# New TensorE prices in a kernel's list scheduler: weight loads counted, durations changed

## The chip, the cores and the metric

The kernel runs on one core of one Trainium2 chip. The time is device microseconds of one execution: the median of three runs before the change is 1827.13 us, with 1824.09 us the lowest and 1828.31 us the highest. Beside the runs there is one profiled execution, whose trace gives every instruction's start and length on each engine: TensorE (PE in the profile, its weight loads PEld), VectorE (DVE), ScalarE (ACT), GpSimd (POOL) and SyncE (SP), which issues all DMA transfers.

## What is computed

One inference step of one encoder layer, on a prompt of 2048 rows and on 8 samples of 16 rows (2176 rows in all), in float32. Cut to what matters:

```python
def mixer_layer(x, mk, mv, shift_prev, rwkv_s0, fox_past, p):
    h = rms_norm(x, norm_g) @ w_in                       # 1024 -> 3654 columns
    fox_cols, rwkv_cols, mem_cols = jnp.split(h, ...)
    o_f = fox_prompt(q, k, v, logf)   # 6 heads x 64, causal, forget gates' running sum on the logits
                                      # (fox_sample: 512 cached rows and 16 new ones)
    xs = token_shift(rwkv_cols, shift_prev, rwkv_mu)
    o_r, s_new, g_r = rwkv_branch(xs, rwkv_s0, ...)  # 6 heads x 64, S <- S diag(w) + S(-kk)^T(a kk) + v^T k
    o_m = mem_attend(mq, mem_q_g, mk, mv)            # 4 heads x 64 into 256 memory rows
    o = jnp.concatenate([o_f * silu(g_f), o_r * silu(g_r), o_m * silu(g_m)], -1)
    return x + o @ w_out, k, v, logf, s_new, rwkv_cols[:, -1:]
```

Outputs are the new rows, the attention keys, values and log forget gates, the memory keys and values, the recurrent states and the last projected rows.

## The kernel before

The work has two stages. The first one (pools `p1`) projects: in four blocks of 512 rows (the first one with the 128 sample rows) it normalises the rows, splits them in a rounded high part and a remainder, and multiplies by the input weights, split likewise, with three products for each pair (tiles `pjd` and `pjt`, 128 rows by 256 to 512 columns, type float32r). Among these products runs the recurrent branch in chunks of 64 rows: small float32 products that use the array in tiles of 64 x 64 or 32 x 32 (`gr`, `gw`, `gx`, `pz`, `pa`), and a chain of 8 steps for each pair of heads and block in which TensorE and VectorE alternate (`sc`, `st`). A plain float32 product makes two passes over the array.

The second one (pools `p2`) attends: for each pair of heads and 512 queries it turns queries and keys (`pt`, transposes on TensorE), finds row maxima (`pm`), computes scores (`pS`), takes the exponent on ScalarE (`P`), splits it (`Ph` on ScalarE, `Pl` on GpSimd) and multiplies by the values (`po`). On the diagonal blocks a bf16 product of a mask with the identity (`idb`) is added to `pm` and `pS`. The samples' attention (`sA` to `sD`, products of 16 columns among them) and the output projection (`py`) are spread among these steps as filler. All of that is in one Python program that only sets which instructions there are.

Their order is not that of the program. `_arrange` (called at the kernel's end) reads all instructions, gives each one a price (`_Op`), and runs a list scheduler (`_schedule`) 18 times: three weights in `_TRIES`, six rounds each, in which the ranks are moved towards the middle between a node's earliest and latest start. The order with the least planned total is taken, for all five engines and so for the order of the DMA transfers on SyncE too. At each step the scheduler takes, over all engines, the candidate with the least key. For TensorE the key comes from `_Array.starts`, a model of the array: it knows the shape of the tiling in use (`self.shape`), when each tile of it is free (`self.free`), a change of tiling (`_TURN`, 92 ns), and a half-clock state (`slow`) in which a product takes twice as long, decided by the work counted in ticks of 3.4 us (`cells`, `_WARM`). `_Array.run` then books the product and says when its result is there. Products of the small tilings that can be run together are one node, a visit (`_visits`). ScalarE, VectorE and GpSimd instructions have a price `time` until the result is seen and `own` until the next one may start; `shares` and `two` say which VectorE instructions wait for GpSimd's at the shared port. A product's times are `own` and, before the change, `time`; in `_Problem.length` and below it `own` also enters the ranks.

Of the kernel before, what the change touches and what calls it, by code (L numbers as in the profile page):

```python
# [1466 lines left out]
_TURN = 92  # L1467
_TICK = 10240 / 3
# [9 lines left out]
class _Pools:  # L1478


    def __init__(self, tc):
        self.tc, self.open, self.below = tc, [], {}
# [10 lines left out]
def _free(dims):  # L1493
    n = 1
    for _, k in dims[1:]:
        n *= k
    return n
# [46 lines left out]
class _Op:  # L1544


    def __init__(self, i, eng):
        ins, outs = ([s.bass_ap for s in x if getattr(s, "bass_ap", None) is not None] for x in (i.ins, i.outs))
        aps, kind = ins + outs, type(i).__name__
        space = lambda a: str(getattr(a.tensor, "_space", ""))  # L1550
        sizes = [_free(list(a.ap)) for a in ins]
        n = max(_free(list(a.ap)) for a in aps)
        self.shares = self.reads = self.two = False
        if eng == "PE":
            x, w = ins[:2]
            wide = str(i.ins[0].dtype) == "dt.float32"
            rows, cols, self.n = list(x.ap)[0][1], sizes[1], sizes[0]
            self.turns, self.plain, self.bf = i.is_transpose, wide and not i.is_transpose, "bf" in str(i.ins[0].dtype)
            size = lambda k: 32 if k <= 32 else 64 if k <= 64 else 128
            self.shape = (size(rows), size(cols)) if self.plain else (128, 128)  # L1560
            self.place = tuple(i.tile_position or (0, 0))
            self.load = 2 * cols / 2.4
            self.cells = self.n * rows / 128 * ((2 if self.turns else 4) if wide else 1)
            if self.plain:
                self.own = 2 * max(cols, self.n) / 1.2 + (10 if rows > 64 else 2)
                self.time = self.own + 165
            else:
                self.own = 30 if self.turns else 40 if self.bf else max(3 + 0.4453 * self.n, 12 + 0.4219 * self.n)
                self.time = 275 if self.turns else self.n / 2.4 + 170
            return  # L1570
        psum = any("PSUM" in space(a) for a in aps)
        scalar = n > 1 and any(k == 1 for k in sizes)
        if eng == "SP":
            size = 4 * list(outs[0].ap)[0][1] * _free(list(outs[0].ap))
            run = min(4 * list(a.ap)[-1][1] if list(a.ap)[-1][0] == 1 else 4 for a in aps)
            self.own, self.wire = (430 if run < 512 else 360), size / 230
            self.time = 1300 + (size / 140 - size / 230) * (run < 1024) / 2
            return
        wide = sum(k > 1 and "SB" in space(a) for k, a in zip(sizes, ins))
        self.reads = wide > 0  # L1580
        if eng == "Activation":
            t = (140 if psum else 178) + 0.833 * n + 90 * scalar
        elif eng == "Pool":
            if "pow" in str(getattr(i, "op", "")):
                t = 360 + 163 * n
            elif "Memset" in kind:
                t = 95 + 0.83 * n
            elif "ScalarPtr" in kind:
                t = 210 + 1.09 * n if n > 256 else 190 + 2.1 * n
            else:  # L1590
                t = 200 + 2.13 * n
        else:
            self.two = not psum and sum(k > 1 for k in sizes) == 1 and ("TensorCopy" in kind or "TensorScalar" in kind)
            self.shares = self.two or wide > 1
            if "Memset" in kind:
                t = max(65, 57 + 1.04 * n)
            elif "Reciprocal" in kind:
                t = 148 + 6.3 * n
            elif "Custom" in kind:
                t = 220 + 1.042 * n  # L1600
            else:
                t = 155 + 0.521 * n if self.two else 152 + 1.042 * n + 52 * (scalar and "ScalarPtr" in kind)
        self.time, self.own = t, t - _BACK[eng]
# [79 lines left out]
class _Array:  # L1683


    def __init__(self):
        self.shape, self.free, self.base, self.last, self.turned, self.cells = None, {}, 0, -1e9, -1e9, {}

    def slow(self, x):
        t = int(x // _TICK)  # L1690
        return 1 if t < 3 or self.cells.get(t - 1, 0) >= _WARM else 2

    def starts(self, c, ready):

        if c.shape == self.shape:
            plain = max(ready, self.base, self.free.get(c.place, 0) if c.shape != (128, 128) else self.free.get(0, 0),
                        self.last + 3)
            if c.turns:
                plain = max(plain, self.turned + 109)
            return plain, plain  # L1700
        plain = max(ready, max(self.free.values(), default=0), self.base)
        return max(ready, max(self.free.values(), default=0) + _TURN, self.base), plain

    def run(self, c, ready):
        s, _ = self.starts(c, ready)
        place = c.place if c.shape != (128, 128) else 0
        w = self.slow(s)
        own = c.own * w
        if c.shape != self.shape:
            self.shape, self.free, self.base = c.shape, {}, s  # L1710
        if c.plain and place not in self.free:
            own += c.load * w
        if c.turns:
            self.turned = s
        self.free[place], self.last = s + own, s
        t0, t1 = s / _TICK, (s + max(own, 1)) / _TICK
# [312 lines left out]
```

## Time and profile before

| | |
|---|---|
| median of three runs | 1827.13 us (1824.09 to 1828.31) |
| profiled execution | 1826.43 us, its span 1824.6 us |
| granted TensorE clock, mean | 0.967 |
| busy: TensorE, weight loads | 1756.1 us (96%), 1395.2 us (76%) |
| busy: VectorE, ScalarE, GpSimd | 927.2, 895.5, 793.7 us |
| DMA | 292.42 MB, mean 160 GB/s |

The span runs from the first to the last instruction; the rest of the execution's time lies around it. TensorE's products are pipelined and their ends in the trace are modelled, so two of them overlap in it and a busy TensorE need not be at its peak: how much a product takes of the engine is read from the distance between starts. The granted clock is 1.0 at full speed and 0.5 at half.

### The profile page before, as it was taken

Reading aid. Unit: us, or ns where it says so; the run is one execution under the profiler, and the core shown is the slowest. Engines: PE = TensorE matmul, PEld = TensorE weight load, DVE = VectorE, ACT = ScalarE, POOL = GpSimd, SP = SyncE. Lnnn points to the kernel's source line nnn. Section 1 sums busy time; section 2 is a strip of 40 time slices with the busy share of each in tenths; the row PEclk is TensorE's granted clock in tenths of the full one; section 3 lists DMA queues with packets and bytes.
Section 4 is the critical chain, followed back from the end, with each engine's and each line's share of the span. In section 5 each row is a group of like instructions: output and inputs, shape, how many; then the busy total and the mean of one; then the engine's idle time right before and its main releaser. Section 6 shows DMA issues by size and latency. Waiting matters only on the chain.

```text
span 1824.6 us, 41978 instructions
## 1 busy us (share of the span) xinstructions
PE 1756.1 (96%) x16883; PEld 1395.2 (76%) x16883; DVE 927.2 (51%) x2102; ACT 895.5 (49%) x1755; POOL 793.7 (43%) x818
## 2 busy tenths in 40 slices
PE   7999999999999999998999998999999999999998
PEld 6998999788877888876788886666666566667776
DVE  5544444464445553545743453767455545575213
ACT  5424343524234323324332434887888477986452
POOL 4555342242131341311332152567676265876452
PEclk8999999999999999999999999899999589999999
DMA  6767463745446464535363353434437542354422
GB/s 193 242 206 242 138 203 113 240 164 174 139 153 203 148 220 163 161 102 178 108 220 131 124 156 120 155 117 156 152 124 242 181 160 87 124 174 145 159 99 97
DMA packets 208905, 292.42 MB, mean 160 GB/s; under 512 B 56844, under 2 KB 161790, under 8 KB 192838
## 3 DMA queue, kind: packets, MB, share of 16 engines
q1 hardware_dynamic: 208710, 289.73, 48.5%
q8 instruction: 133, 2.18, 0.5%
q14 instruction: 62, 0.51, 0.1%
HBM read 202.58 MB, written 87.08 MB: 159 GB/s over the span
## 4 chain that ended last, share of the span: by engine, by line
PE 79%; DVE 7%; ACT 5%; DMA 3%; issue 3%; SPq 1%; POOL 1%; DVEq 0%; ACTq 0%; POOLq 0%
PE pjd L59 20%; PE pjt L59 12%; PE py L59 10%; PE po L59 9%; PE pS L59 7%; PE pm L59 4%; PE sc L59 2%; PE sy L59 1%; PE gr L59 1%; PE pz L59 1%; PE pa L59 1%; PE spr L59 1%; DMA w<-w_d 1%; PE gw L59 1%; PE gx L59 1%
## 5 line engine op out<-in xcount | busy, mean ns | idle before, releaser
L59 PE MATMUL pjd<-xk,w 128*128 128x512 f32 (+4 forms) x2280 | 522.6, 373 | 8.9 <-DVE xk L62 4.1
L59 PEld LDWEIGHTS pjd<-xk,w 128*128 128x128 f32 (+1 forms) x2280 | 380.4, 190 | 75.6 <-issue 10.2
L62 POOL TENSOR_TENSOR Pl<-P,Ph 128x512 fp32r<-128x512 f32 (+3 forms) x272 | 315.4, 1170 | 158.5 <-ACT Ph L1137 122.2
L59 PE MATMUL pjt<-w,xk 128*128 128x256 f32 x2040 | 282.4, 290 | 6.8 <-issue 3.5
L59 PEld LDWEIGHTS pjt<-w,xk 128*128 128x128 f32 x2040 | 260.1, 193 | 16.0 <-issue 7.8
L59 PE MATMUL py<-W,oh 128*128 128x512 f32 x816 | 248.7, 404 | 1.4 <-DVE rb L1179 1.4
L1134 ACT ACTIVATE P<-pS,NB 128x512 f32<-128x512 f32 x240 | 148.7, 623 | 70.8 <-PE pS L59 48.6
L59 PEld LDWEIGHTS py<-W,oh 128*128 128x128 f32 x816 | 150.1, 189 | 40.3 <-DVE rb L1179 1.8
L1078 DVE TENSOR_REDUCE mx<-pm 128x1 f32<-128x512 f32 (+2 forms) x240 | 140.8, 605 | 63.5 <-PE pm L59 60.7
L59 PE MATMUL pS<-Q,K 128*128 128x512 f32 (+1 forms) x480 | 162.6, 397 | 7.8 <-ACT P L1134 3.2
L1137 ACT CAST Ph<-P 128x512 fp32r<-128x512 f32 (+3 forms) x272 | 151.8, 564 | 18.6 <-PE po L59 13.7
L59 PE MATMUL po<-Ph,vt 128*65 128x512 f32 x480 | 156.8, 380 | 0.9 <-ACT ob L1157 0.5
L62 DVE TENSOR_TENSOR xo<-py,xo 128x512 f32<-128x512 f32 x68 | 46.7, 687 | 154.6 <-PE py L59 154.6
L59 PEld LDWEIGHTS pS<-Q,K 128*128 128x128 f32 (+1 forms) x480 | 88.7, 197 | 40.2 <-ACT P L1134 14.0
L62 POOL TENSOR_TENSOR nr<-nr,mhalf 128x8 f32<-128x8 f32 (+2 forms) x43 | 60.9, 1416 | 115.5 <-DVE nr L68 102.0
L59 PE MATMUL pm<-K,Q 67*128 67x512 f32 (+2 forms) x240 | 97.8, 424 | 2.8 <-DVE mx L1078 2.1
L62 POOL TENSOR_TENSOR w<-wraw,w 128x1024 fp32r<-128x1024 f32 (+1 forms) x34 | 79.8, 2348 | 43.8 <-ACT w L197 43.4
L59 PE MATMUL po<-Pl,vt 128*65 128x512 f32 x240 | 90.5, 377 | 0.2
L59 PEld LDWEIGHTS po<-Ph,vt 128*65 128x65 f32 x480 | 64.5, 142 | 26.5 <-issue 3.0
L710 ACT COPY qk<-pjt 128x512 f32<-128x512 f32 (+1 forms) x47 | 26.2, 565 | 102.5 <-PE pjt L59 63.3
L62 POOL TENSOR_TENSOR oh<-ot,oh 128x384 fp32r<-128x384 f32 (+2 forms) x38 | 45.9, 1207 | 61.6 <-ACT oh L1340 51.0
L59 PEld LDWEIGHTS pm<-K,Q 67*128 67x128 f32 x240 | 49.4, 209 | 20.3 <-DVE mx L1078 8.3
(399 smaller groups left out, 2847.4 us busy)
## 6 DMA issues: line engine op xcount, KB each, us to landing
w<-w_d SPq DMA_DIRECT2D x84, 1024.0 KB
w_d<-w SPq DMA_DIRECT2D x28, 1024.0 KB
y_d<-xo SPq DMA_DIRECT2D x21, 512.0 KB
wraw<-in_w_in SPq DMA_DIRECT2D x36, 256.0 KB
xo<-in_x SPq DMA_DIRECT2D x17, 512.0 KB
xo<-y_d SPq DMA_DIRECT2D x17, 512.0 KB
xt<-in_x SPq DMA_DIRECT2D x24, 256.0 KB
xraw<-in_xT SPq DMA_DIRECT2D x24, 256.0 KB
```

Source lines behind the costliest of these rows:

```text
L59: PE.matmul(out, lhsT, rhs, start=start, stop=stop, skip_group_check=True)
L62: e.tensor_tensor(out=out, in0=a, in1=b, op=op)
L710: S.copy(o_, out)
L1078: V.tensor_reduce(out=q["mx"][:, h, t, c0 // 512:c0 // 512 + 1], in_=pm[:, :n], op=MAX, axis=AX.X)
L1134: S.activation(P_[:, c0:], pS[:, c0:], AF.Exp, bias=NB[:, qb, 2 * hp + h, kt:kt + 1] if fox else 0.0)
L1137: S.copy(Ph[:, c0:], P_[:, c0:])
```

## The change

Only the planner's prices and its model of the array are changed. No instruction of the computation is added, removed or resized. What changes in the kernel that runs is the order that the planner finds.

- For products in the 128 x 128 tiling `_Op` now has a price for the weight load (`load`: 109 ns for a transpose, else 9 + 0.85 ns a column) and one for the stream (`stream`: 53 ns for a transpose; columns / 2.4 + 14 ns; for a plain float32 product columns / 2.4 twice, + 2 ns, for each pass). `own` is the larger of stream and load less 11 ns, twice for a plain one. Before, a transpose had 30 ns, a bf16 product 40 ns, a float32r one 0.42 to 0.45 ns a column and 3 to 12 ns.
- `_Array.run` books a load for each pass: it starts when the data is ready and the load ahead of it has gone over to its product (`self.next`), one load ahead of the running product; a bf16 load starts at the earliest 53 ns before the product ahead ends. The product begins when the array is free and its load is done. Results are there 156 ns after the product's end (165 ns in the small tilings).
- `_Array.starts` gives as key, for a product of the tiling in use, the moment at which its load would be done, if it starts at the earliest 118 ns before the array is free. The distance of 109 ns between two transposes (`turned`) is gone. For a change of tiling the key stays without `_TURN`, as before.
- In the small tilings a product's `own` has 10 ns added to its columns' time where it has over 64 rows or 64 columns, 57 ns where it is 32 x 32 or smaller, else 6 ns (before: 10 ns over 64 rows, else 2 ns).
- A ScalarE instruction's price goes up by 15 ns, and by 100 ns where it has a second output (`accum_out`). On VectorE an instruction with two wide operands shares the port only from 61 elements on.

```diff
@@ class _Op
-            if self.plain:
-                self.own = 2 * max(cols, self.n) / 1.2 + (10 if rows > 64 else 2)
-                self.time = self.own + 165
+            if self.shape == (128, 128):
+                self.load = 109 if self.turns else 9 + 0.85 * cols
+                self.stream = 53 if self.turns else (2 if self.plain else 1) * self.n / 2.4 + (2 if self.plain else 14)
+                self.own = (1 + self.plain) * max(self.stream, self.load - 11)
             else:
-                self.own = 30 if self.turns else 40 if self.bf else max(3 + 0.4453 * self.n, 12 + 0.4219 * self.n)
-                self.time = 275 if self.turns else self.n / 2.4 + 170
+                self.own = 2 * max(cols, self.n) / 1.2 + (10 if rows > 64 or self.n == 64 else 57 if rows <= 32 and cols <= 32 else 6)
...
-            t = (140 if psum else 178) + 0.833 * n + 90 * scalar
+            t = (155 if psum else 193) + 0.833 * n + 90 * scalar + 100 * (len(outs) > 1)
...
-            self.shares = self.two or wide > 1
+            self.shares = self.two or wide > 1 and n > 60
@@ class _Array
+    def loads(self, c, ready):
+        return max(ready, self.next, self.free[0] - 53 if c.bf else 0)
+
     def starts(self, c, ready):
-        if c.shape == self.shape:
-            plain = max(ready, self.base, self.free.get(c.place, 0) if c.shape != (128, 128) else self.free.get(0, 0),
-                        self.last + 3)
-            if c.turns:
-                plain = max(plain, self.turned + 109)
-            return plain, plain
-        plain = max(ready, max(self.free.values(), default=0), self.base)
-        return max(ready, max(self.free.values(), default=0) + _TURN, self.base), plain
+        end = max(self.free.values(), default=0)
+        if c.shape != self.shape:
+            return max(ready, end + _TURN, self.base), max(ready, end, self.base)
+        if c.shape == (128, 128):
+            s = max(ready, end, self.last + 3)
+            return s, max(s, max(ready, end - 118) + c.load)
+        s = max(ready, self.base, self.free.get(c.place, 0), self.last + 3)
+        return s, s
...
+        if c.shape == (128, 128):
+            for _ in range(1 + c.plain):
+                load = self.loads(c, ready)
+                begin = max(s, self.free[0], load + c.load * w)
+                self.next = max(load + (c.load - 11) * w, begin)
+                self.free[0] = begin + c.stream * w
+            till = self.free[0]
+        else:
+            till = self.free[c.place] = s + (c.own + (c.load if c.place not in self.free else 0)) * w
...
-        return s, s + (own - c.own) + c.time + (w - 1) * c.own
+        return s, till + (156 if c.shape == (128, 128) else 165)
```

More of the change, by code (lines that the diff above doesn't have):

```diff
@@ L1686, in __init__ @@
     def __init__(self):
-        self.shape, self.free, self.base, self.last, self.turned, self.cells = None, {}, 0, -1e9, -1e9, {}
+        self.shape, self.free, self.base, self.last, self.cells, self.next = None, {}, 0, -1e9, {}, 0
     def slow(self, x):
@@ L1704, in run @@
+        return s, s
     def run(self, c, ready):
         s, _ = self.starts(c, ready)
-        place = c.place if c.shape != (128, 128) else 0
         w = self.slow(s)
-        own = c.own * w
         if c.shape != self.shape:
[L1710 to L1716, printed above, removed]
+            self.shape, self.free, self.base, self.next = c.shape, {}, s, s
+            if c.shape == (128, 128):
+                self.free[0] = s
@@ new lines, in run @@
+        if c.shape == (128, 128):
+            for _ in range(1 + c.plain):
[6 more added lines that the diff above has]
+            till = self.free[c.place] = s + (c.own + (c.load if c.place not in self.free else 0)) * w
+        self.last = s
+        t0, t1 = s / _TICK, max(till, s + 1) / _TICK
```

## The prediction

> **What bounds the kernel now.** I read the page's first lines, then the table of 50 us stretches, then what ended TensorE's idle time, and last TensorE's own order in a few stretches.
>
> ```profile
> span 1824.6 us, 41978 instructions
> PE 1756.1 (96%) x16883; PEld 1395.2 (76%) x16883; DVE 927.2 (51%) x2102; ACT 895.5 (49%) x1755; POOL 793.7 (43%) x818
> ...
> PE 79%; DVE 7%; ACT 5%; DMA 3%; issue 3%; SPq 1%; POOL 1%; DVEq 0%; ACTq 0%; POOLq 0%
> ```
>
> TensorE is busy for 1756.1 of 1824.6 us and is 79% of the chain that ended last; no other engine passes 51%. So 68.5 us is all that a better order can win back as idle time, and beside it only what TensorE loses while it counts as busy: a halved clock, a weight load that nothing covers, a change of the array's tiling. Columns below: busy time (instructions) of PE, PEld, DVE, ACT and POOL, granted clock, DMA share, GB/s.
>
> ```profile
> 0.00:50.00 50.00, 39.62 (x181) 34.61 (x182) 29.85 (x69) 29.03 (x65) 23.05 (x34) 0.90 0.70 210
> ...
> 1100.00:1150.00 50.00, 40.79 (x466) 31.49 (x458) 23.51 (x51) 23.48 (x45) 11.08 (x20) 0.85 0.37 118
> ...
> 1400.00:1450.00 50.00, 45.53 (x293) 30.96 (x292) 31.02 (x74) 24.90 (x51) 14.69 (x20) 0.65 0.58 190
> 1450.00:1500.00 50.00, 48.39 (x324) 31.62 (x323) 24.79 (x51) 35.75 (x67) 30.65 (x31) 0.80 0.55 192
> ...
> 1800.00:1824.60 24.60, 18.68 (x77) 13.85 (x76) 16.00 (x21) 1.84 (x4) 2.60 (x4) 1.00 0.30 118
> ```
>
> Three places hold idle time that is not a matter of order among many ready products: the start (50 - 39.62 = 10.4 us, nothing has arrived yet), the change from the projection stage to the attention stage (50 - 40.79 = 9.2 us) and the last 24.6 us (5.9 us). They make 25.5 us, so **43.0 us** of idle time lie scattered over the rest. Their causes:
>
> ```profile
> PE gx L59 <- issue: 6.1, 5, 1.9
> PE pjd L59 <- DVE xk L62: 4.1, 3, 2.5
> PE pq L59 <- ACT xsq L247: 3.6, 2, 3.3
> PE pjt L59 <- issue: 3.5, 2, 3.0
> ```
>
> These are the four largest entries (total us, times, longest); the largest is 6.1 us. No single wait is there to be removed.
>
> **The change part by part.** No instruction is added, removed or resized; the planner's prices change, so the order of all five engines' streams, SP's transfers among them, is drawn anew.
>
> *Long products.* Most of TensorE's time is long products; the two costliest groups alone hold 805 us:
>
> ```profile
> L59 PE MATMUL pjd<-xk,w 128*128 128x512 f32 (+4 forms) x2280 | 522.6, 373 | 8.9 <-DVE xk L62 4.1
> ...
> L59 PE MATMUL pjt<-w,xk 128*128 128x256 f32 x2040 | 282.4, 290 | 6.8 <-issue 3.5
> ```
>
> The chain shows their pitch (start, length, what, count):
>
> ```profile
> 99.33 8.29 PE pjt L59 x69
> ...
> 679.16 9.32 PE pjd L59 x40
> ```
>
> 8.29 / 69 = 120 ns for 256 columns and 9.32 / 40 = 233 ns for 512. The old price gives max(3 + 0.4453 x 256, 12 + 0.4219 x 256) = 120 and 231; the new one 256 / 2.4 + 14 = 121 and 227. Both fit: for the bulk the edit is worth 0. The premise that a load hides behind the running product is borne out too: a 128-column load is priced at 9 + 0.85 x 128 = 118 ns and would not fit into the 120 ns pitch beside 256 / 2.4 = 107 ns of streaming unless it ran under the product before. The Trainium skill speaks against that: "TensorE: Matmul & The Clock Gate", Part 3, section The mechanism, lets a load overlap a running product only when their row groups differ. By that rule each of these full-height products would take about 107 + 118 = 225 ns, the new model would be wrong everywhere, and the time would be case C's below; the 120 ns row contradicts it.
>
> *Transposes.* From TensorE's order in the projection stage (start, length, what):
>
> ```profile
> 1118.80 0.28 PE L748 MATMUL ptok<-ident,tsb 128*128 128x128 f32 x1
> 1118.84 0.48 PE L59 MATMUL pjd<-xk,w 128*128 128x512 f32 x1
> 1119.15 0.27 PE L748 MATMUL ptok<-ident,tsb 128*128 128x128 f32 x1
> 1119.18 0.48 PE L59 MATMUL pjd<-xk,w 128*128 128x512 f32 x1
> 1119.50 0.27 PE L748 MATMUL ptok<-ident,tsb 128*128 128x128 f32 x1
> ```
>
> One transpose and one 512-column product take 0.35 us, so the transpose costs 350 - 233 = 117 ns. The old price was 30 ns (109 only when two followed each other). The new one lets the next product's load start when the transpose starts: 118 ns. That correction is right and worth 87 ns each. With the count of
>
> ```profile
> L998 PE MATMUL pt<-ident,tok 128*128 128x128 f32 x132 | 33.2, 306 | 3.0 <-DMA tok<-q_d 2.8
> ...
> L1280 PE MATMUL pt3b<-ident,sD 128*128 128x128 f32 x38 | 10.9, 322 | 2.1 <-DVE sD L68 1.8 <-ACT sD L1281 0.2
> ```
>
> 170 transposes x 87 ns = 15 us of TensorE time that the old plan did not see, nearly all in the attention stage.
>
> *The bf16 mask products.*
>
> ```profile
> 1203.70 0.40 PE L59 MATMUL pS<-Q,K 65*128 65x512 f32 x1
> 1203.94 0.23 PE L59 MATMUL pS<-negT,idb 128*128 128x128 bf16 x1
> 1203.98 0.43 PE L59 MATMUL po<-Ph,vt 128*65 128x512 f32 x1
> 1204.25 0.40 PE L59 MATMUL pm<-K,Q 67*128 67x512 f32 x1
> ```
>
> ```profile
> L59 PEld LDWEIGHTS <-idb 128*128 128x128 bf16 x192 | 19.2, 102 | 28.2 <-issue 23.7
> ```
>
> From 1203.70 to 1204.25 run two 512-column products and a mask: 550 - 2 x 233 = 84 ns for the mask. Old price 40. New: the load may start 53 ns before the product ahead ends, takes 118, the mask streams 67, and the next load starts only with the mask, so the next product starts 183 ns after the one ahead ended. The old price is 44 ns too low, the new one 99 ns too high; over 192 masks the plan's error goes from -8 us to +19 us. This part of the correction overshoots.
>
> None of these corrections makes TensorE itself faster: 170 transposes still cost 117 ns. They change what the planner thinks is ready when, and the key by which it picks: a 128-row product is now keyed at max(end of the running one, its release + 118), so one whose data has only just arrived is passed over for one that has lain ready. I see three terms.
>
> (1) Idle time: 43.0 us is the upper bound, 0 the lower. Where there is stock TensorE is kept full (150.00 of 150 us):
>
> ```profile
> 1500.00:1650.00 150.00, 143.60 (x965) 95.12 (x964) 92.08 (x175) 123.31 (x235) 106.05 (x107) 0.98 0.43 143
> 1650.00:1800.00 150.00, 150.00 (x692) 111.88 (x689) 37.71 (x59) 74.80 (x128) 84.14 (x70) 1.00 0.34 115
> ```
>
> but many small waits on chains (PE to ACT to PE) come back in any order. I take a third: -14 us.
>
> (2) Loads that start only when data arrives. TensorE's load side waited
>
> ```profile
> PEld pS L59 <- ACT P L1134: 17.4, 47, 1.1
> ...
> PEld pm L59 <- DVE mx L1078: 8.3, 21, 1.0
> ```
>
> 68 times; each exposes at most 118 ns, 8 us in all, 0 if the order finds nothing else. A third again: -3 us.
>
> (3) Changes of tiling. The new key charges a just-released 128-row product but not a change of tiling, so more visits to the small tilings are possible. A visit of 64-row products:
>
> ```profile
> 1109.70 1.09 PE L59 MATMUL pjd<-xk,w 128*128 128x512 f32 x4
> 1110.72 1.15 PE L59 MATMUL pa<-bt,za 64*64 64x64 f32 x32
> ```
>
> Four products at 233 ns end at 1110.63, the visit starts 0.09 us later; entering and leaving is about 0.2 us. Thirty more visits would cost 6 us, none 0; I take +3.
>
> The corrections of ScalarE (+15 ns an instruction, +100 with a second output) and of VectorE's port sharing act on engines at half load and cost nothing while TensorE's work covers them; without that cover the plan's 1755 ScalarE instructions are worth at most 26 us of ScalarE time that it sees and that was there before. SP's transfers are moved with the products; the DMA share of the 50 us rows shown is 0.30 to 0.70, so I cost their shifts at 0, though a 10 us row below reaches 1.01 and transfers that bunch there would be late.
>
> Sum: -14 - 3 + 3 = -14 on the profiled execution's 1826.4 us (span 1824.6 and 1.8 around it): 1812.4. The median of the runs is 0.7 above that execution: **1813 us**.
>
> **The rivals.** The clock decides most of them. Around 1400 us (ten-microsecond stretches, columns as above):
>
> ```profile
> 1410.00:1420.00 10.00, 7.94 (x36) 3.96 (x34) 8.78 (x19) 6.90 (x14) 3.57 (x7) 0.75 0.88 271
> 1420.00:1430.00 10.00, 9.11 (x28) 4.57 (x28) 2.82 (x9) 4.03 (x8) 2.50 (x4) 0.50 0.23 61
> 1430.00:1440.00 10.00, 8.53 (x42) 5.92 (x42) 8.15 (x21) 5.18 (x11) 1.51 (x2) 0.50 0.50 158
> 1440.00:1450.00 10.00, 10.00 (x133) 8.96 (x132) 3.61 (x9) 0.00 (x0) 0.21 (x1) 0.50 0.37 114
> 1450.00:1460.00 10.00, 9.02 (x36) 5.63 (x38) 5.87 (x10) 6.44 (x11) 5.55 (x5) 0.67 1.01 361
> 1460.00:1470.00 10.00, 9.95 (x30) 4.86 (x23) 6.15 (x16) 3.32 (x8) 3.21 (x4) 0.52 0.38 118
> ```
>
> A stretch with 2 us idle opens it, and for 60 us the clock stands near half: 2.5 + 5 + 5 + 5 + 3.3 + 4.8 = 25.6 us of full-clock time.
>
> *A. The half-clock stretch closes too.* Then 25.6 us more are won: 1813 - 26 = 1787. For it: one idle spell of 2 us opens it, and a shifted order need not have that spell. Against: the products that keep it going (narrow sample products) remain, and nothing in the edit looks ahead at the clock. The Trainium skill, in the same page's Part 1, section HAM oscillation, has the clock halve after an idle gap over about 3.4 us; TensorE's idle time between 1410 and 1420 was 2.06 us in all and the clock fell nevertheless, so the trace disagrees. By that rule this stretch would be at full clock before and after.
>
> *B. Slower: the stock runs out early and the clock halves a second time.* The new key favours products that have lain ready, which are projections and sample products, over just-released scores and values. The stock that now fills 1650 to 1800 without a gap is used earlier, and a later stretch is left with PE-to-ACT chains alone. Price: one more stretch like the one shown, +25.6; with the -14 still had elsewhere +11.6, 1839; without, 1853. It decides from the point where a ten-microsecond stretch after 1500 us holds TensorE under 8 us busy. For it: 1500 to 1650 already idles 6.4 us with ScalarE at 82%, the mask overshoot distorts just that stage, and a plan's order that was best by one set of prices need not be so by another. Against: the prices of transposes, the larger error, become right.
>
> *C. No change.* All 16883 products still run, TensorE is 96% busy, the bulk's price did not move, and the redrawn idle time comes out as before: 1827.
>
> *D. The change does not do what it says.* For masks it does not: 84 ns measured, 40 before, 183 after. If that weighs as much as the transposes, the plan is as far off as before, and the result is C.
>
> **How the numbers follow.** A measurement of this kernel tells about 0.2% (3.7 us) from no change. Forecast 0.42 (its own range 1799 to 1823, from all three terms at a doubled or no gain), A 0.18, B 0.27, C with D 0.13. So faster 0.42 + 0.18 = 0.60, same 0.13, slower 0.27. The range reaches from 5 us beyond A, 1782, to halfway between B's two times, 1846; I leave about 1 in 10 below and 1 in 10 above.
>
> **What would show it.** Right: the 50 us table has the scattered idle time down from 43 to about 29 us, the transposes and masks at the same 117 and 84 ns, and the half-clock stretch still there, perhaps elsewhere. Wrong towards A: mean granted clock above 0.98. Wrong towards B: a ten-microsecond stretch after 1500 us with TensorE under 8 us and clock 0.5, and 1650 to 1800 no longer full. If the time moves while idle time and clock do not, the order changed how often the array is retiled or how the loads are covered, and my first term was the wrong one.

## The result, and the profile after

The changed kernel takes 1855.51 us (median of four runs, 1853.35 to 1856.23) against 1826.89 us for the kernel before: a ratio of 1.0157, with an interval of 1.0139 to 1.0174. It is 28.6 us slower. 1813 us had been forecast, with 1846 us as the upper end.

The page of the changed kernel, its span, its engines and the shares of the chain that ended last:

```profile
span 1854.5 us, 41966 instructions
PE 1769.7 (95%) x16883; PEld 1407.9 (76%) x16883; DVE 929.9 (50%) x2102; ACT 894.8 (48%) x1755; POOL 790.9 (43%) x818
...
PE 67%; DVE 10%; ACT 6%; issue 4%; POOL 3%; DMA 3%; SPq 1%; DVEq 0%; POOLq 0%; ACTq 0%
```

TensorE is busy 13.6 us longer and idle for 84.8 us, where it was 68.5 us, and its share of the chain fell from 79% to 67%. The same stretches as in the prediction, of the changed kernel (busy time and instructions of PE, PEld, DVE, ACT and POOL, granted clock, DMA share, GB/s):

```profile
0.00:50.00 50.00, 38.04 (x163) 32.75 (x164) 24.52 (x58) 29.57 (x68) 21.72 (x31) 1.00 0.69 197
1120.00:1170.00 50.00, 40.44 (x415) 31.32 (x411) 23.25 (x50) 22.16 (x43) 11.99 (x21) 0.77 0.37 115
1150.00:1200.00 50.00, 40.51 (x150) 26.66 (x150) 35.88 (x65) 33.50 (x65) 16.83 (x26) 0.59 0.53 164
...
1450.00:1500.00 50.00, 45.24 (x294) 31.43 (x294) 27.61 (x63) 28.05 (x54) 20.09 (x21) 0.67 0.54 178
...
1650.00:1800.00 150.00, 148.24 (x697) 110.03 (x697) 59.80 (x91) 85.10 (x149) 92.06 (x77) 1.00 0.45 151
...
1829.90:1854.50 24.60, 18.72 (x81) 14.75 (x80) 15.63 (x21) 1.84 (x4) 2.20 (x3) 0.98 0.30 118
```

The three places that have no stock of work idle 12.0, 9.6 (1120 to 1170) and 5.9 us, much as before. The scattered idle time is 84.8 - 27.4 = 57.4 us, where it was 43.0: it went up by the 14 us by which it was to go down.

Next the span cut at the first transpose of queries (`pt`), which starts at 1131.4 us before and at 1151.2 us after. Before:

```profile
0.00:1131.40 1131.40, 1090.46 (x13322) 935.12 (x13323) 565.89 (x1453) 414.89 (x870) 376.84 (x417) 0.98 0.52 169
1131.40:1824.60 693.20, 665.61 (x3564) 460.07 (x3562) 361.29 (x650) 480.57 (x885) 416.84 (x402) 0.94 0.44 146
```

After:

```profile
0.00:1151.20 1151.20, 1098.18 (x13322) 940.64 (x13323) 568.89 (x1454) 417.10 (x873) 378.70 (x420) 0.99 0.51 166
1151.20:1854.50 703.30, 671.56 (x3562) 467.27 (x3562) 361.01 (x649) 477.67 (x882) 412.20 (x399) 0.93 0.44 144
```

The projection stage lost 19.8 us and the attention stage 10.1 us. They are losses of two kinds, which the clock tells apart. I call a stretch's time multiplied by its mean granted clock its **full-clock time**: what it would take if the clock never fell and nothing else moved. With the clock taken to three places, the attention stage has 693.2 x 0.941 = 652 us before and 703.3 x 0.927 = 652 us after: no difference. So the attention stage, where nearly all of the prediction's price corrections lie, lost by the clock alone.

The projection stage has 1113 us before and 1137 us after by the same sum, but this sum leaves something out. The clock record of each trace begins with a switch to full speed, at 25.8 us before and at 48.1 us after, and what lies ahead of it counts as 1.00. TensorE's products show otherwise (start, length, what, idle time before). Before, first at a recorded 1.0, then at a recorded 0.5:

```profile
27.96 1.72 PE L59 MATMUL pjd<-xk,w 128*70 128x384 f32 x8 [0.70 <-ACT xk L275]
...
36.06 2.38 PE L59 MATMUL pjd<-xk,w 128*70 128x384 f32 x6 [2.50 <-DVE xk L62]
```

After, and the ten microseconds in which the first of these lines lies:

```profile
33.72 3.53 PE L59 MATMUL pjd<-xk,w 128*70 128x384 f32 x9
...
40.84 2.19 PE L59 MATMUL pjd<-xk,w 128*70 128x384 f32 x6 [1.69 <-DVE xk L62]
```

```profile
30.00:40.00 10.00, 5.65 (x15) 2.72 (x15) 9.36 (x18) 8.97 (x21) 4.67 (x3) 1.00 0.41 132
```

Eight such products take 1.72 us at full clock and six take 2.38 us at half; in the kernel after nine take 3.53 us, so the clock is half there, though the view gives 1.00. With the time ahead of the record taken at half clock, which is an estimate, the projection stage has 1100 us at full clock before and 1113 us after: 13 us more, close to the 12 us by which TensorE's idle time there grew (53.0 us, where it was 40.9). The order got worse there by so much; the other 6 us of the stage's 19.8 are half clock, in the first 50 us.

Most of the stage's loss is there by the end of the second block of rows, where both kernels have the same count of TensorE's instructions behind them. Before and after:

```profile
0.00:561.80 561.80, 540.14 (x6256) 479.79 (x6257) 280.69 (x705) 216.95 (x453) 218.04 (x239) 0.98 0.56 183
```

```profile
0.00:579.30 579.30, 549.08 (x6255) 484.54 (x6256) 283.06 (x705) 218.17 (x453) 220.41 (x239) 0.99 0.54 177
```

The kernel after is 17.5 us late there: 8.6 us by idle time (30.2 us instead of 21.7) and 8.9 us because TensorE is busy longer for the same count, which fits the longer half clock at the start. Of the idle time, 6.1 us came in the second block alone. Before and after:

```profile
313.50:561.80 248.30, 246.12 (x3039) 204.30 (x3032) 129.03 (x346) 87.72 (x185) 69.17 (x89) 1.00 0.52 170
```

```profile
320.30:579.30 259.00, 250.72 (x3082) 206.65 (x3082) 131.99 (x345) 88.04 (x185) 70.08 (x89) 0.99 0.49 162
```

In this block no single wait stands out. TensorE's largest waits in it, after (us, times, longest); before there are two, of 1.7 and 0.3 us:

```profile
PE pjd L59 <- issue: 2.1, 1, 2.1
PE sc L59 <- DVE st L65: 1.5, 1, 1.5
PE gx L59 <- issue: 1.4, 1, 1.4
PE pjd L59 <- DVE xsk L65: 1.1, 2, 0.7
```

The chain of waits through the block, before and after (shares by line):

```profile
by line: PE pjd L59 39.1%; PE pjt L59 16.8%; DMA w<-w_d 4.8%; PE sc L59 4.4%; PE sy L59 2.8%; PE gr L59 2.7%; PE pa L59 2.5%; PE spr L59 2.4%; issue 2.2%; PE pss L59 1.5%; PE pz L59 1.5%; PE gx L59 1.4%; PE pmv L59 1.2%; PE gw L59 1.2%; PE 
```

```profile
by line: PE pjd L59 32.7%; PE pjt L59 12.9%; PE sc L59 4.1%; issue 3.9%; DVE yt L62 3.2%; DVE ytmp L62 2.9%; PE sy L59 2.7%; PE pa L59 2.3%; PE pz L59 2.2%; PE spr L59 1.9%; PE gr L59 1.8%; PE pbt L59 1.5%; PE gw L59 1.5%; PE gx L59 1.5%; S
```

The long products carry 56% of it before and 46% after, where the recurrent branch's inverse of small triangular tiles on VectorE (`yt`, `ytmp`) has come in with 6%. So I read the idle part as many short waits, for this branch among others; it was not tested apart.

### The profile page after: what moved, and what is told of

It reads as the page before. It is cut to its first block, busy times and chain, and to the rows that moved or that the text cites. A ratio compares the mean times of both kernels' runs of the same rounds, so it can differ in the third digit from the quotient of the medians.

```text
span 1854.5 us, 41966 instructions
## 1 busy us (share of the span) xinstructions
PE 1769.7 (95%) x16883; PEld 1407.9 (76%) x16883; DVE 929.9 (50%) x2102; ACT 894.8 (48%) x1755; POOL 790.9 (43%) x818
## 4 chain that ended last, share of the span: by engine, by line
PE 67%; DVE 10%; ACT 6%; issue 4%; POOL 3%; DMA 3%; SPq 1%; DVEq 0%; POOLq 0%; ACTq 0%
PE pjd L59 17%; PE py L59 9%; PE po L59 8%; PE pjt L59 8%; PE pS L59 6%; PE pm L59 3%; PE sc L59 2%; DVE ytmp L62 2%; POOL Pl L62 2%; DVE yt L62 2%; PE sy L59 1%; PE pa L59 1%; PE pz L59 1%; PE gr L59 1%; SPq L456 1%
## 5 line engine op out<-in xcount | busy, mean ns | idle before, releaser
L59 PE MATMUL pjd<-xk,w 128*128 128x512 f32 (+5 forms) x2280 | 529.7, 375 | 20.6 <-issue 6.2
L59 PEld LDWEIGHTS pjd<-xk,w 128*128 128x128 f32 (+1 forms) x2280 | 384.4, 191 | 85.0 <-issue 16.6
L59 PE MATMUL pjt<-w,xk 128*128 128x256 f32 x2040 | 289.4, 289 | 0.0
L59 PE MATMUL pS<-Q,K 128*128 128x512 f32 (+2 forms) x480 | 167.1, 399 | 10.2 <-ACT P L1134 5.5
L59 PE MATMUL po<-Ph,vt 128*65 128x512 f32 x480 | 160.6, 385 | 2.6 <-ACT ob L1160 1.7
L59 PEld LDWEIGHTS pm<-K,Q 67*128 67x128 f32 x240 | 50.1, 210 | 27.4 <-DVE mx L1078 12.1
L62 POOL TENSOR_TENSOR oh<-ot,oh 128x384 fp32r<-128x384 f32 (+2 forms) x38 | 44.4, 1170 | 56.2 <-ACT oh L1340 42.2
```

What stands on the lines that cost most here:

```text
L59: PE.matmul(out, lhsT, rhs, start=start, stop=stop, skip_group_check=True)
L62: e.tensor_tensor(out=out, in0=a, in1=b, op=op)
```

## Experiments

The change has three parts that can be put back one by one: the model of the array for the 128 x 128 tiling (loads, streams, the key in `starts`), the price `own` of the small tilings (below the small price), and the prices of ScalarE and VectorE. The theories: the order is redrawn, and any such edit moves the time by as much, whatever it corrects (lottery, L); the fault lies in the array's model as a whole (P) or in all the rest (R); in the key (K); in the overpriced mask (M); in ScalarE's prices (A); in the small price (T); or in the weight of `_TRIES` from which the winning plan comes (W): its stream of before is the one that 0.3 alone gives, and that of after the one that 0.6 alone gives.

All runs. The ratio stands against runs of the kernel before on the same chip. The clock and the full-clock time are medians over a kernel's runs, by the clock as recorded, with the range of the second. The last column is for the profiled execution alone: its span less half of all time at half clock, with the time ahead of the clock record counted as half. That record begins between 25.7 and 33.3 us in all traces but those of after (48.1) and after_old_engines (51.5); the four executions of after, within 3 us of each other, have recorded clocks of 0.961 twice and 0.965 twice, as if the record began late in two of them:

| kernel | us | ratio (95%) | clock | full-clock us | profiled, start at half |
|---|---|---|---|---|---|
| before (57 runs) | 1828.3 | | 0.965 | 1766 (1760-1774) | 1752 |
| after | 1855.5 | 1.0157 (1.0139-1.0174) | 0.963 | 1787 (1781-1791) | 1765 |
| before_turn91 | 1848.1 | 1.0102 (1.0046-1.0157) | 0.954 | 1764 (1762-1766) | 1751 |
| before_turn93 | 1831.9 | 1.0017 (0.9991-1.0043) | 0.967 | 1771 (1765-1773) | 1756 |
| after_turn91 | 1861.8 | 1.0176 (1.0111-1.0241) | 0.963 | 1793 (1792-1794) | 1778 |
| after_turn93 | 1857.6 | 1.0153 (1.0098-1.0208) | 0.962 | 1787 (1787-1787) | 1771 |
| pe_model_only | 1830.4 | 1.0016 (0.9976-1.0057) | 0.969 | 1774 (1768-1778) | 1759 |
| rest_only | 1834.3 | 1.0047 (0.9995-1.0098) | 0.965 | 1770 (1765-1775) | 1748 |
| after_old_key | 1841.7 | 1.0055 (1.0020-1.0091) | 0.970 | 1789 (1784-1793) | 1769 |
| after_mask_load | 1854.0 | 1.0120 (0.9984-1.0257) | 0.962 | 1784 (1783-1784) | 1767 |
| after_old_tiles | 1837.6 | 1.0049 (1.0031-1.0067) | 0.968 | 1779 (1775-1785) | 1766 |
| after_old_engines | 1852.3 | 1.0121 (1.0051-1.0192) | 0.968 | 1792 (1785-1799) | 1772 |
| after_weight_03 | 1843.4 | 1.0078 (1.0031-1.0126) | 0.972 | 1791 (1790-1793) | 1776 |
| before_weight_06 | 1853.8 | 1.0130 (1.0071-1.0188) | 0.958 | 1775 (1774-1776) | 1760 |
| after_tile32_17 | 1848.9 | 1.0109 (1.0036-1.0182) | 0.962 | 1780 (1779-1780) | 1764 |
| after_tile32_17_93 | 1852.8 | 1.0122 (1.0065-1.0178) | 0.960 | 1778 (1777-1779) | 1762 |
| after_old_64 | 1835.2 | 1.0045 (1.0022-1.0068) | 0.968 | 1775 (1772-1781) | 1761 |
| after_old_64_93 | 1853.3 | 1.0124 (1.0068-1.0181) | 0.967 | 1792 (1791-1794) | 1774 |
| after_corrected | 1842.9 | 1.0078 (1.0027-1.0130) | 0.963 | 1775 (1772-1782) | 1757 |
| after_corrected_93 | 1843.1 | 1.0090 (1.0052-1.0128) | 0.968 | 1783 (1781-1785) | 1769 |

### Is it the luck of the order?

The price of a change of tiling is moved by 1 ns, which corrects nothing and redraws the order; once up and once down, in both kernels:

```diff
-_TURN = 92
+_TURN = 91   (or 93)
```

> The kernel before, with the planner's price of a change of tiling at 91 ns instead of 92: an edit too small to be right or wrong, so it only draws another order. Theory L (before's order was a lucky draw among orders that the old prices find, and any redrawing loses it): slower than before by 0.5 to 2%, 1836 to 1862 us. Theory S (the new prices and the new key themselves lead to worse orders): within 0.4% of before, 1820 to 1834 us.

> The same with 93 ns. Theory L: 1836 to 1862 us, and another time than the order with 91 ns has. Theory S: 1820 to 1834 us.

> The changed kernel, with a change of tiling at 91 ns instead of 92. Theory L: any time in 1825 to 1870 us, the two nudged orders some 10 us or more apart, overlapping with the nudged orders of the kernel before. Theory S: 1848 to 1862 us, close to the changed kernel's 1855.5, above all nudged orders of before.

> The same with 93 ns. Theory L: 1825 to 1870 us, overlapping with the nudged orders of before. Theory S: 1848 to 1862 us.

One nanosecond costs the kernel before 1.0% in one direction and nothing in the other; both plans of after stay 1.5 to 1.8% slower. The first number by itself would make a lottery of 29 us believable. The clock says what it was. Of the kernel before with 91, in two stretches:

```profile
1150.00:1200.00 50.00, 43.52 (x196) 30.91 (x195) 38.54 (x73) 37.87 (x74) 23.66 (x36) 0.66 0.55 170
...
1450.00:1500.00 50.00, 46.42 (x288) 31.06 (x286) 27.18 (x62) 22.09 (x43) 14.50 (x17) 0.66 0.55 176
```

It has two half-clock stretches, as after has, and a mean clock of 0.954; its full-clock time, 1764 us, is that of before. So an edit that corrects nothing moves the time by 20 us **through the clock**, and that part is a lottery. The full-clock time is steadier: 1764, 1766 and 1771 by the record for three plans of before, 1787, 1787 and 1793 for three of after. With the start at half clock they are 1751, 1752 and 1756 against 1765, 1771 and 1778. The two groups stay apart, but by 9 us at the nearest, and further below a nudge of 1 ns moves the full-clock time of one plan by 13 us. So three plans each make a luckier order of before unlikely; they don't rule it out.

### One part alone

pe_model_only is after with both other parts put back; rest_only is before with these two parts:

```diff
# pe_model_only (against after)
-                self.own = 2 * max(cols, self.n) / 1.2 + (10 if rows > 64 or self.n == 64 else 57 if rows <= 32 and cols <= 32 else 6)
+                self.own = 2 * max(cols, self.n) / 1.2 + (10 if rows > 64 else 2)
-            t = (155 if psum else 193) + 0.833 * n + 90 * scalar + 100 * (len(outs) > 1)
+            t = (140 if psum else 178) + 0.833 * n + 90 * scalar
-            self.shares = self.two or wide > 1 and n > 60
+            self.shares = self.two or wide > 1
# after_old_key (against after), in _Array.starts
-            return s, max(s, max(ready, end - 118) + c.load)
+            return s, s
# after_mask_load (against after), in _Array.loads
-        return max(ready, self.next, self.free[0] - 53 if c.bf else 0)
+        return max(ready, self.next)
```

> The changed kernel with the prices of ScalarE, VectorE's port sharing and the small tilings put back: only the model of the 128 x 128 tiling (loads, streams, key) is new. Theory P (the array model or its key loses the time): 1848 to 1865 us, as the changed kernel. Theory R (the other engines' and the small tilings' prices lose it): 1825 to 1840 us, as the kernel before and its nudged order with 93 ns. Theory L (a lottery of about 10 us either way on top): 1835 to 1850 us.

> The kernel before with only those other prices new (ScalarE +15 and +100 ns, sharing from 61 elements, small tilings). Theory P: 1825 to 1842 us. Theory R: 1848 to 1865 us. Theory L: 1830 to 1850 us.

> The changed kernel with the key put back: a product of the tiling in use is keyed at the moment the array is free and its data is there, without the load. All prices stay new. Theory K (the key that passes over just-released products delays the recurrent branch's chains): 1822 to 1840 us. If prices lose the time: 1848 to 1865 us.

> The changed kernel without the rule that a bf16 load starts at the earliest 53 ns before the product ahead ends: a mask is then priced at 118 ns, nearer to the 84 measured than 183. Theory M (the overshoot on the masks loses time): the attention stage, from the first transpose of queries to the end, becomes shorter than the changed kernel's 703 us by 10 us or more, 1845 us or less in all. Otherwise 1850 to 1865 us, since masks stand only in the attention stage and 20 of the 30 us are lost before it.

Neither half alone does it, with one plan of each: 1.0016 and 1.0047, both intervals holding 1, with 1774 and 1770 us at full clock (1759 and 1748 with the start at half). P and R fall as single causes. The two stages of pe_model_only:

```profile
0.00:1130.70 1130.70, 1088.50 (x13322) 934.33 (x13323) 564.91 (x1450) 414.82 (x870) 370.27 (x414) 0.99 0.52 169
1130.70:1827.50 696.80, 665.91 (x3564) 461.42 (x3561) 358.87 (x653) 481.83 (x885) 416.30 (x404) 0.94 0.44 146
```

With the whole new model of loads and streams, the projection stage is as short as before (1130.7 against 1131.4 us) and idles 42.2 us.

The old key gives 1841.7 us, which neither theory had forecast. It brings 14 us back in time, but by its clock (0.970); at full clock it stays at 1789 us (1769 with the start at half), so K falls. With the mask's rule taken out, the median is 1854.0 us with an interval too wide to say more; its attention stage takes 703.4 us against 703.3, and its full-clock time is 1784 us (1767). The overpriced mask is not the cause, and M falls.

### After with one part put back, and the winning weight

after_old_tiles puts back only the first line of the diff above, after_old_engines only the other two. The weights:

```diff
-_TRIES = ((0.3, 0), (0.45, 0), (0.6, 0))
+_TRIES = ((0.3, 0),)   # after_weight_03;  ((0.6, 0),) in before_weight_06
```

> The changed kernel with the small tilings' price put back. I now read two numbers: the time, and time x mean granted clock (the full-clock time), which in one kernel's runs stays within about 5 us while the time moves with the clock. It is 1764 to 1774 us for the kernel before, its nudged orders and the two partial edits, 1784 to 1793 us for everything with both halves of the change. Theory T (the dearer visits of the small tilings, together with the array model, delay the recurrent branch): full-clock time 1765 to 1776. Theory A (ScalarE's price does, with the array model): 1784 to 1793.

> The changed kernel with ScalarE's prices and VectorE's port sharing put back, the small tilings' price new. Theory T: full-clock time 1784 to 1793. Theory A: 1765 to 1776.

> The changed kernel, but only the six rounds with the first weight (0.3) are tried, which is the weight of the order that the prices of before chose; the new prices chose 0.6. Theory W (the new prices choose among the 18 orders wrongly): full-clock time 1765 to 1776 us and 1822 to 1842 us in all. If the orders are all alike under the new prices: 1784 to 1793 full-clock.

> The kernel before, but only the six rounds with weight 0.6 are tried. Theory W: full-clock time 1784 to 1793 us, 1845 us or more in all. Otherwise 1764 to 1774 full-clock, as the nudged order with 91 ns, which also has weight 0.6 and 1764.

The small price alone, put back, leaves 1.0049 and 1779 us; ScalarE's and VectorE's prices put back leave 1.0121 and 1792 us. A falls. T had 1765 to 1776, so 1779 lies outside both ranges. The two stages of after_old_tiles:

```profile
0.00:1139.70 1139.70, 1092.67 (x13322) 937.47 (x13322) 575.35 (x1454) 414.02 (x871) 384.57 (x417) 0.99 0.51 168
1139.70:1831.60 691.90, 661.71 (x3562) 456.74 (x3562) 360.15 (x648) 479.85 (x884) 411.81 (x402) 0.95 0.44 146
```

11.5 of the projection stage's 19.8 us are back, but at full clock, with the start at half, only 4 of 13: 1109 us, where after has 1113 and before 1100. Over both stages this plan is no better than after (1766 against 1765 us). So T is not shown by this run. The weight changes places with the clock again: before's plan of 0.6 is slow (1.0130) at 0.958 with 1775 us at full clock, 1 us above the range for "otherwise", and after's plan of 0.3 is less slow at 0.972 with 1791 us. W falls.

### What of the small price is wrong

The new price can be set against the trace, visit by visit. In the kernel before, visits of 64-column products:

```profile
1110.72 1.15 PE L59 MATMUL pa<-bt,za 64*64 64x64 f32 x32
1111.70 1.10 PE L59 MATMUL pa<-gm,za 64*64 64x64 f32 x32
1112.73 1.15 PE L59 MATMUL sc<-su,bt 128*64 128x64 f32 x32
```

These 64 instructions of `pa` are 32 products, since each makes two passes, 16 in a row at each of two places of the array. They take 2.01 us, leaving included (some 0.09 us, the prediction's row). The old price is 16 x (106.7 + 2) + 53 = 1.79 us, the new one 16 x (106.7 + 10) + 53 = 1.92 us: with leaving, 2.01. This half is right. In the kernel after, a visit of 32 x 32 products:

```profile
241.36 0.69 PE L59 MATMUL gx<-x,gm 32*32 32x32 f32 x32
241.98 0.98 PE L59 MATMUL pjd<-xk,w 128*128 128x384 f32 x4
245.19 0.44 PE L59 MATMUL pjd<-xk,w 128*128 128x384 f32 x1 [2.23 <-issue]
```

These 32 instructions are 16 products, 8 in a row at each of two places; they take 0.62 us, 0.53 without leaving. Visits of 64 instructions at four places (`gw`) took 0.68 us, 0.59 without. The old price is 8 x (53.3 + 2) + 27 = 0.47 us, the new one 8 x (53.3 + 57) + 27 = 0.91 us. This half overshoots by more than the old price was short; 17 ns in place of 57 would give 0.59, right for `gw` and high for `gx`. So I tried each half by itself, and all prices as measured:

```diff
# after_tile32_17 (with _TURN = 93: after_tile32_17_93)
-... + (10 if rows > 64 or self.n == 64 else 57 if rows <= 32 and cols <= 32 else 6)
+... + (10 if rows > 64 or self.n == 64 else 17 if rows <= 32 and cols <= 32 else 6)
# after_old_64 (with _TURN = 93: after_old_64_93)
+... + (10 if rows > 64 else 57 if rows <= 32 and cols <= 32 else 2)
# after_corrected (with _TURN = 93: after_corrected_93): 17 as above, no mask rule as above, and
-_BACK = {"DVE": 85, "Activation": 85, "Pool": 50}
+_BACK = {"DVE": 85, "Activation": 100, "Pool": 50}
```

> The changed kernel with 17 ns instead of 57 added to a 32 x 32 product. The trace of before has a visit of 64 such instructions (32 products, 8 on each of 4 places) take 0.59 us without the change of tiling, that is 8 x (53.3 + 17) + 27 ns; the old price gave 0.47, the new one gives 0.91. Theory T32 (this overshoot, together with the array model, loses the full-clock time): 1765 to 1779 us full-clock. Theory T64 (the +10 ns for 64 columns does): 1784 to 1793.

> The changed kernel with the old price of the 64 x 64 products and the new 57 ns for the 32 x 32 ones. Theory T32: full-clock time 1784 to 1793 us. Theory T64: 1765 to 1779.

> The changed kernel with three prices moved to what the trace shows: 17 ns for 32 x 32 products, no rule for bf16 loads (a mask at 118 ns, 84 to 128 measured), and ScalarE's +15 ns kept for when a result is seen but taken out of when the next instruction may start (the trace has 483 ns from start to start where the old price had 481). If right prices give good orders: full-clock time 1755 to 1770 us, the same as before or better. If the order found is a draw that the prices' last errors do not decide: 1765 to 1785.

> The same with a change of tiling at 93 ns, another draw. If right prices give good orders: 1755 to 1770 us full-clock; if it is a draw: 1765 to 1785, and some 8 us or more from the one with 92.

> The changed kernel with 17 ns for 32 x 32 products and a change of tiling at 93 ns: a second draw of the order with only the 64-column term wholly new. If each of the two terms alone loses about half, full-clock time 1775 to 1783 us, as the first draw's 1780. If the first draw was luck and the 64-column term loses it all: 1784 to 1793. If the 32 x 32 overshoot loses it all: 1765 to 1774.

> The changed kernel with the old price for 64-column products, 57 ns for 32 x 32 ones, and a change of tiling at 93 ns: a second draw of the other half. If each term loses about half: 1775 to 1783 us full-clock, as the first draw's 1775. If the 32 x 32 term loses it all: 1784 to 1793. If the 64-column term loses it all: 1765 to 1774.

17 ns: 1780 us at full clock, between the ranges of T32 and T64, and 1778 us in the second plan, as if each term lost about half. The old 64-column price: 1775 us in one plan and 1792 us in the other (1761 and 1774 with the start at half), one as T64 and one as T32 has it, so nothing can be said of that half. All prices as measured: 1775 and 1783 us (1757 and 1769), as an order that is a draw would have it. The better of the two is as good at full clock as plans of before; in time none beats the kernel before.

**What the runs show together.** Where the array's model or the whole small price is the old one, full-clock times by the record are 1764, 1766, 1770, 1771, 1774, 1775 and 1779 us (seven plans); where both are new, but for one line of the model in after_old_key and after_mask_load, 1784, 1787, 1787, 1789, 1791, 1792 and 1793 us (seven plans). With the start at half clock the gap closes: 1748 to 1766 us, 1756 in the mean, against 1765 to 1778, 1771 in the mean. The line was drawn after seeing the numbers, and the small price in the old model stands on one plan alone (rest_only). The four plans in which only one half of the small price was changed, and the two with all prices as measured, spread over both, 1757 to 1774.

What stands firmest is a comparison within one set of prices: four plans of before's prices (three of `_TURN`, and the weight 0.6) have 1751 to 1760 us, four of after's (three of `_TURN`, and the weight 0.3) 1765 to 1778. So the new prices together gave worse orders, by about 17 us in the mean at full clock. That it takes two parts together is supported, since each alone gave a plan like those of before, but it isn't shown: a 1 ns nudge moved two of the kernels by 13 us, and the parts stand on one or two plans each.

**What stays open.** Why the new prices make worse orders isn't settled: by the visits measured, one half of the new small price is right and the other too high, yet the measured value gets back only a part. Nor is it settled which part counts, or through which wait.

## Why the prediction was wrong

**The step that failed** is the first term: truer prices were to mean less idle time, -14 us of it. The runs showed more idle time, in a worse order. A part of the loss that no term had is the half clock.

**Term 1, idle time: -14 us forecast, +14 us measured.** It stood on the step from "that correction is right" to "less idle time". The first half holds. Transposes between 512-column products, after:

```profile
1137.62 0.28 PE L748 MATMUL ptok<-ident,tsb 128*128 128x128 f32 x1
1137.66 0.48 PE L59 MATMUL pjd<-xk,w 128*128 128x512 f32 x1
1137.98 0.27 PE L748 MATMUL ptok<-ident,tsb 128*128 128x128 f32 x1
```

360 - 233 = 127 ns, near the 117 ns read before. The sum of 15 us was somewhat high: of the 170 transposes in the kernel before, 45 are followed by another one, for which the old price was 109 ns already, so 125 x 87 = 11 us were unseen. The second half failed: pe_model_only has these true prices and wins nothing (1774 us at full clock against 1766), and after_corrected, with every price that I could measure, is 0.8% slower than before. Here truer prices did not make better plans: all 20 plans leave 37 to 60 us of idle time in the projection stage, and how much varies from plan to plan. The lower bound of the term, "0", had no reason behind it; the orders drawn here all idle about as much as before's or more, and the range had no side for that.

**The missing term.** The prediction corrected four prices (long products, transposes, masks, changes of tiling) and listed "three terms". The edit of the small price, in the same diff, was given no cost, neither a price against the rows nor a bound. Whether it has a part in the loss stays open, as said above. It could have been priced: the row of 32 `pa` instructions was quoted for another purpose, and the visit that it begins gives the 2.01 us above.

**Term 2, late loads: -3 us forecast.** After, the load side waits (us, times, longest):

```profile
PEld pS L59 <- ACT P L1134: 16.7, 31, 2.4
...
PEld pm L59 <- DVE mx L1078: 12.4, 33, 1.2
```

64 times instead of 68, for 29.1 us instead of 25.7: no gain.

**Term 3, changes of tiling: +3 us forecast.** There are some 500 changes before and about 11 more after. 11 more at about 0.1 us each are 1 us: small, as costed.

**Bulk at 0, masks as rival D.** The long products kept their pitch (the chain of after):

```profile
124.94 7.44 PE pjt L59 x62
```

7.44 / 62 = 120 ns, so the bulk's edit was worth 0. That the mask overshoots is right in size, but as a cause it falls with after_mask_load. ScalarE's and VectorE's prices were costed at 0, and after_old_engines agrees. SyncE's shifts were costed at 0 too; loads did move (those of the small weights are issued from 11.15 us on instead of 8.30), and what that cost was not separated.

**The rivals.** A falls: the clock did not rise, 0.965 against 0.967 in the profiled executions. B named the right side, more half clock as a part of it, and the time (1839 or 1853), this last by chance: its mechanism is not what the trace shows. Its stretch was to come after 1500 us, from stock used early; 1650 to 1800 us is nearly as full as before (148.24 of 150), and the attention stage needs the same 652 us at full clock. What grew is the half-clock stretch at the change of the stages: by the clock records it lasts from 1150.6 to 1188.2 us after, and from 1135.1 to 1155.6 us before. In after, ten-microsecond stretches and TensorE's order:

```profile
1150.00:1160.00 10.00, 4.05 (x16) 3.09 (x17) 5.11 (x9) 6.16 (x12) 3.27 (x8) 0.53 0.99 307
1160.00:1170.00 10.00, 8.31 (x30) 5.07 (x28) 9.57 (x20) 7.27 (x12) 1.00 (x1) 0.50 0.48 155
```

```profile
1151.15 1.09 PE L998 MATMUL pt<-ident,tok 128*128 128x128 f32 x4 [2.15 <-DVE gth L65]
1152.83 1.12 PE L998 MATMUL pt<-ident,tok 128*128 128x128 f32 x4 [0.59 <-DMA tok<-q_d]
1158.15 1.11 PE L59 MATMUL pS<-Q,K 128*128 128x512 f32 x2 [4.20 <-DVE Q L62]
```

A mean of 0.53 over ten microseconds leaves at most 0.6 us of it at full speed, so the clock had fallen by 1150.6, in the 2.15 us gap and before the 4.20 us one. The Trainium skill, "TensorE: Matmul & The Clock Gate", Part 1, section HAM oscillation, puts the limit at idle gaps over some 3.4 us; here too the clock fell earlier than that. Just ahead of this gap lie only 0.52 us of work and another gap, of 0.92 us, so whether the length of one gap or the share of idle time decides is not shown. B's price was too high: with the start, the time lost to half clock rose from 73 to 89 us in the profiled executions, by 17 us and not by 25.6.

**In sum.** The profiled executions' spans differ by 29.9 us (the medians by 28.6). About 13 us of it are the worse order of the projection stage, which goes with the new prices. The other 17 us are half clock, 10 of them in the attention stage, and look like luck of the order: over the four plans of before this loss runs from 63 to 96 us, and over the four of after from 69 to 89.

## What to carry to other kernels

When a planner's prices change, every edit in the diff needs a price against the trace, and the redrawn order a range on both sides of zero: here new prices, in part truer, gave plans from 0.2% to 1.8% slower. Multiply time by the mean granted clock before two orders are compared: it took away a 20 us difference that a 1 ns edit had made. Look first from when on the clock is recorded: the unrecorded start made 24 us out of 13 here. Before an order is credited or blamed, draw it again, more than once, with an edit that means nothing.

## What the runs showed of the hardware

One and the same program (the kernel before, 57 runs) takes 1818.2 to 1842.4 us, and the time follows the granted clock, 0.972 to 0.958, while its product stays within 1760 to 1774 us. The same 16883 instructions of TensorE lose between 52 us (after_weight_03) and 84 us (before_turn91) to recorded half clock, by their order; the start comes on top.

TensorE's waits on "issue" of 1.4 to 2.7 us in the projection stage after, such as the 2.23 us before 245.19 above, follow transfers of instructions. In that stretch after there is one:

```profile
q8 instruction: 1, 0.02, 1.8%
```

It starts at 242.6 us, and five more such waits (ending at 325.6, 443.6, 593.1, 857.4 and 1118.8 us) have a transfer of the same kind 2.2 to 2.6 us ahead of their ends. All six lie among or next to visits of many short products. That the transfer causes the wait is inferred from this timing and wasn't tested; 104 such transfers start in the projection stage, and six of them are followed by such a wait. In idle time all "issue" waits of TensorE make 11.0 us before and 13.2 us after. But the clock falls with five of the six (records at 246.1, 444.0, 594.2, 857.1 and 1119.9 us, each for 3.4 or 6.8 us), though the gaps are no longer than 2.7 us. Behind the gap of 1.4 us that ends at 443.6 us stand 6.8 us at half clock, which cost 3.4 us: more than the gap itself.
